# The last down projection of each MLP in seven products instead of eight, with six more adding transfers a layer and the two gate products behind it computed side by side

## The chip, the cores and the metric

One core of a Trainium2 chip runs the whole program. The metric is the device time of one execution, in microseconds (us). The kernel before was executed three times for its time: 1659.44, 1661.74 and 1659.78 us, a median of 1659.78 us. One further execution was recorded by the hardware profiler: all rows shown here come from it.

Five engines work beside each other: TensorE (PE) does matrix products and loads their weights (PEld), VectorE (DVE), ScalarE (ACT) and GpSimd (POOL) work on elements, and SyncE (SP) starts the transfers from memory. POOL's queue starts transfers too, here those that add to what lies at their destination. Each engine runs its own list of instructions in order, and waits where an instruction needs something that another engine has not finished.

## The reference

Two requests of 512 and 256 tokens go through two encoder layers with the same weights. Layer 0 mixes tokens by windowed attention, layer 1 by a gated short convolution. Behind either mixer stand an MLP with squared ReLU and a gated input embedding:

```python
for i in range(DEPTH):                       # DEPTH = 2, D_MODEL = 1024, D_FF = 4096
    ...                                      # x = x + attention or short convolution
    h = rms_norm(x, norm_mlp[i])
    x = x + jnp.square(jax.nn.relu(h @ mlp_w_up[i])) @ mlp_w_down[i]
    gate = jax.nn.sigmoid(rms_norm(x, norm_ple[i]) @ ple_w_gate[i])
    x = x + (p[i] @ ple_w_proj[i]) * gate    # p[i]: 256 features per token
return rms_norm(x, final_norm)
```

Everything is float32. The change lies in the end of the MLP, `... @ mlp_w_down[i]`, and in the beginning of `gate`, in both layers.

## The kernel before

**Layout.** The activations lie transposed: `x(m)`, m = 0..7, is a tile of 128 features by 768 tokens (both requests side by side). `H` = 384 is half the tokens, and a matmul of the MLP has 128 x 128 weights and 384 columns. A product in float32 is made from high and low parts: the high part is a copy in the shorter type fp32r (written by ACT), the low part is the difference to the original (usually a subtraction by DVE). Three matmuls stand for one: high x high, high x low of the activations, low of the weights x high.

**MLP.** The 4096 hidden rows are cut into 8 groups of 512. A group has two *up chunks* (`up`, u = 0..15), and two halves of a *down* projection (`down(g, h)`), h naming the half of the output rows. The jobs run up 0, up 1, then for each group up, down half 0, down half 1, up, so that the down projection of a group stands two chunks behind its up projection. The last job is `last_down`, group 7.

**Seven products.** Up chunks and the down projections of groups 0 to 6 cut a product of 2 x 2 blocks into seven block products instead of eight. Their keys are `w11, s3, s2, w12, s1, w22, s4`: `w` keys are blocks of the weights, `s` keys are sums of blocks (`sums32`, `sums14`, on DVE). `QS7` gives the activations that each meets (blocks or sums as well, made by `Acts`: `highx`, `lowx`, `t13`, `t42`, `high`, `low`). `product7` issues one product into one PSUM bank: in a down half a key takes 12 matmuls, six for each of its two banks. Results of one key are used twice: into another bank by a copy on ACT (`copies`: banks `A` into `C` behind w11, `A` into `B` behind s2), where the next key then accumulates. `added` in `down` adds the finished banks to `x` on DVE.

**Weights.** `Weights7` fetches two chunks of the weights (`wraw`, 512 KB each, by SP) for one half, makes high parts on ACT (`high`) and low parts on DVE (`low`; `split` does both). For the key w22 alone the low part is made without DVE (`added` of `Weights7`, line 446): ACT copies the high part negated, and a transfer on POOL's queue adds the original from memory to it. Tiles named `whi`, `wlo` have two buffers, `vhi`, `vlo` (w22) and `zhi`, `zlo` (s3 and s2) one, as have the two sums.

**The last group.** `last_down` does the whole of group 7 without the scheme: the activations of the two last up chunks are kept as they are (`whole`), four chunks of weights are fetched and split one after the other (`weight`), and each gives two output blocks of 24 matmuls: 192 matmuls of 384 columns a layer, all at line 131. Each finished block is added to `x(m)`, and `nxt.block` begins the next norm with it: ACT makes the scaled high part `xs_ple`, DVE the low part, ACT the square, DVE its running sum.

**The gates.** In layer 0 `ple` goes through eight gate products `gate` over all 768 tokens, each with its own 512 KB of weights. Behind the first stands the sum of squares over the 128 rows (a matmul), from which `rstd_ple` comes, and then for each gate a chain of DVE and ACT steps adds its part to `x`. In layer 1 `last_ple` does the same for 512 tokens first and 256 behind them, with the weights kept, and ends with the final norm. The first two gates stand ahead of the sum of squares there.

**What sets the order.** Inside the MLP the lists of ACT, PE and DVE are written by hand (`manual_schedule`): an instruction runs in the order in which the code names it. `late()` takes the next deferred step from a list (`pend`), which spreads the work on the activations of a chunk over the next chunk. Transfers on SP and POOL start in the order of the code as soon as their buffers are free.

Of the kernel before, what the change touches and what calls it, by code (L numbers as in the profile page):

```python
# [18 lines left out]
P = 128  # L19
D = 1024  # L20
KB = D // P
# [26 lines left out]
def trunk_kernel(ctx: ExitStack, tc: tile.TileContext, a: dict, out: bass.AP):  # L48
# [124 lines left out]
    class Norm:  # L173
# [4 lines left out]
        def __init__(self, i, name, places, acc, rstd=None):  # L178
            self.i, self.name, self.places, self.rplace = i, name, places, rstd
            self.xs = [], []  # L180
            self.acc = slot(acc, f"acc_{name}", F32)[:, : self.n]

        def block(self, m, xb):
            g = gain(self.i, m)
            hi, lo = (slot(self.places[8 * p + m], f"xs_{self.name}") for p in range(2))
            self.xs[0].append(hi[:])
            self.xs[1].append(lo[:])
            act.activation(hi[:], xb, AF.Copy, scale=g)
            dve.scalar_tensor_tensor(lo[:], xb, g, hi[:].bitcast(F32), ALU.mult, ALU.subtract)
            self.square(m, xb)  # L190
# [214 lines left out]
    class Weights7:  # L405
# [44 lines left out]
        def added(self, group):  # L450
# [6 lines left out]
            nc.gpsimd.dma_start(lo[:], src[:, src.shape[1] - lo.shape[1] :], accum_op=ALU.add)  # L457

# [586 lines left out]
    def mlp(l, norm, nxt, w, places, early, product=None, begun=None):  # L1045
# [14 lines left out]
        def acts_of(u, y1, y2, rest):  # L1060

            own = places[7 * (u % 2) : 7 * (u % 2) + 7]
            e = Acts(y1, y2, own, groups[u // 2], u % 2)
            if u < 2 * NG - 2:
                return [
                    lambda: squared(rest),
                    lambda: e.highx(0),
                    lambda: (e.highx(1), e.lowx(0), e.lowx(1), e.t13()),
                    e.t42,
                    lambda: e.high(0),  # L1070
                    lambda: e.high(1),
                    lambda: e.low(0),
                    lambda: e.low(1),
                ]

            def whole(i, q):
                hi, lo = slot(own[2 * i], "act"), slot(own[2 * i + 1], "act")
                split(hi[:], lo[:], q[:])
                groups[u // 2].setdefault("whole", {})[u % 2, i] = hi[:], lo[:]

            return [lambda: squared(rest), lambda: whole(1, y2), lambda: whole(0, y1)]
# [22 lines left out]
        def up_begun(u, w, make, then):  # L1104
# [71 lines left out]
        def up_plain(u, w, make, then):  # L1176
# [91 lines left out]
        def up(u, w, make, then):  # L1268


            first = u == PLAIN[l]
# [25 lines left out]
            if seven:  # L1297
                v.sums14()
                v.high("s32")
# [7 lines left out]
            rectified(y1, c, 0, H, ALU.max)  # L1307
            late()
            if seven:
                v.low("direct")  # L1310
            else:
                v = [then(0)]
# [8 lines left out]
            pend.extend(acts_of(u, y1, y2, y1))  # L1321
            return v

        def down(g, h, w, make, then):

            xg = groups[g]
            top, low = ([x(4 * h + 2 * i + s) for s in range(2)] for i in range(2))

            def products(ts, key, start):
                for s, t in enumerate(ts):  # L1330
                    product7(t, w, key, xg, start, 2 * P, s * P)
# [10 lines left out]

            w.low("s32")
# [9 lines left out]
            b = [bank("B", "b")[:, :H] for _ in range(2)]  # L1353
            products(b, "s3", True)
            p = big("p")
            for i in range(2):
                act.activation(p[:, i * H : i * H + H], b[i], AF.Copy)
            products(a, "s2", False)
            d = copies("B", a)
            for i in range(2):  # L1360
                t = low[i].rearrange("p (a n) -> p a n", a=2)
                q = p[:, None, i * H : i * H + H].broadcast_to([P, 2, H])
                dve.tensor_tensor(t, t, q, ALU.subtract)
# [621 lines left out]
```

## Time and profile before

| What | Value |
|---|---|
| median of three executions | 1659.78 us (1659.44 to 1661.74) |
| profiled execution | 1661.51 us |
| its span, first to last instruction | 1659.5 us |
| mean granted TensorE clock | 0.996 |
| matmuls on PE | 9414 |
| last down of layer 0 | about 749.9 to 783.3 us |
| its gates (`ple`) | from 783.3 us |
| last down of layer 1 | about 1543.2 to 1576.8 us |
| its gates (`last_ple`) and the end | from 1576.8 to 1659.5 us |

In rows of the profile the engine's name is followed by the line of the code, the operation and `out<-in` with the shape of each; `x12` is a count. A bracket `[1.07 <-ACT xs L312]` says that the engine had waited 1.07 us ahead of the instruction, and for which instruction of which engine. In a table of stretches each row gives the start and end, the length, and then the busy time of PE, PEld, DVE, ACT and POOL with the number of instructions, the granted clock in parts of full speed, the mean busy share of the transfer engines and GB/s. Groups of instructions show busy time, mean ns of one, and the idle time ahead of them. A row of transfers gives the queue, the count, the size and the us from issue to landing.

### The profile page before, as it was taken

The page shows a single profiled execution, that of the slowest core. Times are in us where ns is not written, and L with a number is a line of the kernel's source. Part 1 is how long each engine was busy: PE and PEld are TensorE (multiplying, and loading weights), DVE is VectorE, ACT ScalarE, POOL GpSimd, SP SyncE. Part 2 cuts the span into 40 slices and gives each one's busy share as a digit, 9 for nine tenths or more (in the row PEclk, how much of TensorE's full clock was granted, in tenths as well). Part 3 has the DMA queues.
Part 4 walks back from the last instruction along what each step waited for, and adds up shares of the span by engine and source line. Part 5 has one row for each costly group of instructions (what it writes and reads, how often), then busy time and mean ns, then how long its engine had stood idle before and what let it go on. Part 6 is the DMA issues. An engine that isn't in the chain of part 4 may idle for free.

```text
span 1659.5 us, 24297 instructions
## 1 busy us (share of the span) xinstructions
PE 1637.6 (99%) x9414; PEld 1587.3 (96%) x9414; DVE 1380.8 (83%) x2242; ACT 948.5 (57%) x1508; POOL 71.7 (4%) x104
## 2 busy tenths in 40 slices
PE   8999999999999999999999999999999999999997
PEld 7988789999999999999999999999999999999986
DVE  7598888898889889877888777778889888988776
ACT  7377766865556556545654434555555655655554
POOL 0211000000000000000000000000000000000000
PEclk9999999999999999999999999999999999999998
DMA  8755322443233333242312222112333323333222
GB/s 267 199 154 149 87 64 83 121 109 87 83 86 96 96 96 91 71 122 69 98 62 77 76 77 76 64 64 73 87 96 96 95 87 79 90 96 108 69 87 99
DMA packets 55476, 161.11 MB, mean 97 GB/s; under 512 B 7056, under 2 KB 10128, under 8 KB 55360
## 3 DMA queue, kind: packets, MB, share of 16 engines
q1 hardware_dynamic: 45184, 139.89, 26.4%
q0 software_dynamic: 10176, 19.67, 6.7%
q8 instruction: 74, 1.21, 0.3%
q14 instruction: 42, 0.34, 0.1%
HBM read 138.82 MB, written 10.48 MB: 90 GB/s over the span
## 4 chain that ended last, share of the span: by engine, by line
PE 88%; DVE 7%; ACT 4%; issue 1%; DMA 0%; DVEq 0%; SPq 0%; ACTq 0%
PE a L486 33%; PE mm L131 10%; PE mm L140 8%; PE b L486 8%; PE d L486 5%; PE c L486 5%; PE B L486 4%; PE C L486 4%; PE gate L140 3%; PE pt L760 1%; PE p L1096 1%; PE p L1199 1%; PE gate L131 1%; PE O L770 1%; PE O L771 1%
## 5 line engine op out<-in xcount | busy, mean ns | idle before, releaser
L486 PE MATMUL a<-xs,whi 128*128 128x384 f32 x624 | 121.8, 337 | 0.0
L444 ACT ACTIVATE vhi<-wraw 128x512 fp32r<-128x512 f32 x67 | 42.2, 631 | 132.3 <-PE B L486 87.9
L486 PEld LDWEIGHTS a<-xs,whi 128*128 128x128 f32 x624 | 110.0, 188 | 0.2 <-DVE y L1306 0.2
L486 PE MATMUL a<-t,zhi 128*128 128x384 f32 x536 | 109.1, 337 | 0.0
L486 PE MATMUL a<-t,whi 128*128 128x384 f32 x536 | 108.8, 336 | 0.0
L486 PE MATMUL b<-t,zhi 128*128 128x384 f32 x536 | 108.7, 336 | 0.0
L1341 DVE TENSOR_TENSOR x<-x,a 128x384 f32<-128x384 f32 x112 | 62.1, 554 | 55.3 <-PE a L486 55.3
L486 PE MATMUL a<-act,whi 128*128 128x384 f32 x448 | 96.5, 337 | 0.0
L486 PEld LDWEIGHTS a<-t,whi 128*128 128x128 f32 x536 | 94.9, 188 | 0.0
L486 PEld LDWEIGHTS b<-t,zhi 128*128 128x128 f32 x536 | 94.9, 188 | 0.0
L486 PEld LDWEIGHTS a<-t,zhi 128*128 128x128 f32 x536 | 94.8, 188 | 0.0
L464 DVE TENSOR_TENSOR wlo<-wraw,whi 128x1024 fp32r<-128x1024 f32 x70 | 85.2, 1218 | 7.9 <-ACT whi L444 7.9
L444 ACT ACTIVATE whi<-sum 128x1024 fp32r<-128x1024 f32 x67 | 70.6, 1054 | 27.0 <-PE a L486 22.7
L464 DVE TENSOR_TENSOR wlo<-sum,whi 128x1024 fp32r<-128x1024 f32 x67 | 81.8, 1220 | 5.1 <-ACT whi L444 5.1
L1058 ACT ACTIVATE y<-y 128x768 f32<-128x768 f32 x64 | 53.7, 839 | 54.4 <-DVE y L1055 54.3
L464 DVE TENSOR_TENSOR zlo<-sum,zhi 128x1024 fp32r<-128x1024 f32 x67 | 81.5, 1217 | 0.0
L140 PE MATMUL mm<-xs_mix,whi 128*128 128x512 f32 (+1 forms) x320 | 81.0, 341 | 0.0
L486 PEld LDWEIGHTS a<-act,whi 128*128 128x128 f32 x448 | 79.8, 188 | 0.0
L444 ACT ACTIVATE whi<-wraw 128x1024 fp32r<-128x1024 f32 x72 | 75.7, 1051 | 7.0 <-PE C L486 7.0
L444 ACT ACTIVATE zhi<-sum 128x1024 fp32r<-128x1024 f32 x67 | 70.9, 1058 | 11.9 <-DVE sum L420 11.0
L486 PE MATMUL a<-xs,wlo 128*128 128x384 f32 x312 | 67.1, 336 | 0.0
L358 ACT ACTIVATE t<-y 128x768 fp32r<-128x768 f32 x56 | 45.7, 838 | 34.9 <-DVE y L349 34.4
(345 smaller groups left out, 4558.4 us busy)
## 6 DMA issues: line engine op xcount, KB each, us to landing
wraw<-in_up SPq DMA_DIRECT2D x64, 512.0 KB, 3.9
wraw<-in_down SPq DMA_DIRECT2D x64, 512.0 KB, 4.2
wraw<-in_w_in SPq DMA_DIRECT2D x24, 512.0 KB, 3.5
wraw<-in_gate SPq DMA_DIRECT2D x16, 512.0 KB, 3.4
vlo<-in_up POOLq DMA_DIRECT2D x28, 256.0 KB, 5.6
vlo<-in_down POOLq DMA_DIRECT2D x28, 256.0 KB, 6.0
pj<-pjs SPq DMA_DIRECT2D x16, 384.0 KB, 2.8
wraw<-in_w_q SPq DMA_DIRECT2D x8, 512.0 KB, 4.6
```

The lines of the kernel that those rows point to most:

```text
L131: pe.matmul(t, lhsT=w, rhs=x[:, o:e], start=first and i == 0 and j == 0, stop=last and i == n - 1 and j == 2)
L140: pe.matmul(ps[:, o:e], lhsT=w, rhs=x[:, o:e], start=i == 0 and j == 0, stop=i == n - 1 and j == 2,)
L358: act.activation(t[0][:], (self.q1, self.q2)[i][:], AF.Copy)
L444: act.activation(hi[:], src, AF.Copy)
L464: dve.tensor_tensor(lo[:], src, hi[:].bitcast(F32), ALU.subtract)
L486: pe.matmul(ps, lhsT=a, rhs=b, start=start and i == 0, stop=i == len(terms) - 1, skip_group_check=True)
L760: pe.transpose(pt[:, h * P : (h + 1) * P], lg[h // 2][:, h % 2, b * P : (b + 1) * P], ident[:],)
L770: pe.matmul(O[:], lhsT=v, rhs=ph[:], start=b == 0, stop=False)
L771: pe.matmul(O[:], lhsT=v, rhs=pl[:], start=False, stop=b == nk - 1)
L1058: act.activation(t[:], t[:], AF.Square)
L1096: pe.matmul(ps[o], lhsT=wt[:, c], rhs=xs[f"x{h + 1}{1 + o}"][m][part], start=k == 0 and j == 0, stop=k == KB - 1 and j == 2,)
L1341: dve.tensor_tensor(t[:, o : o + H], t[:, o : o + H], f, op)
```

## The change

`last_down` is gone. Group 7 becomes two more halves of the seven products, written out in two new functions, `down_first` (half 0) and `down_last` (half 1), with an order of their own. The activations of the last two chunks are made by `Acts` as elsewhere, those of chunk 15 inside the last `up` and the first half. A layer does 2 x 7 x 12 = 168 matmuls there.

- The order of the keys in both halves is w11, w12, s3, s2, s1, w22, s4 (an ordinary half has w11, s3, s2, w12, s1, w22, s4).
- Inside a key the matmuls go chunk by chunk of the activations, over both banks in turn: four with the first chunk's high and low part, two with the low part of the weights, then the second chunk, which has the weights' low part first and the activations' low part last. Before, one bank was finished and then the other.
- `down_first` has the weights for its half prepared by the last `up`; the low part for w11 and w12 is subtracted by DVE late in that `up`.
- Low parts by adding transfers, in both layers: the sum for s3 and s2 of half 0 (`sum_added`, from the sum itself), w11 and w12 of half 1 (`v.added("direct")`), w22 of both halves, and the whole weights of the first two gates (`weight_added`). Those of w22 are 256 KB, the four others 512 KB.
- Each block's `xs_ple` high and low part is made as its `x(m)` becomes final: blocks 0 to 3 while half 1 runs, 6 behind its key w22, then 7, 4 and 5. `nxt.block` is cut into `high`, `low` and `square` for that.
- `first_gates` computes the two first gates side by side: blocks 0 to 3 of the first gate, then of the second, then blocks 6 and 7 of both, then 4 and 5. The sum of squares stands ahead of the second gate's last part in layer 0, and behind the third gate in layer 1. `ple` and `last_ple` take over from there.
- `last_ple` has its kept weights and outputs in other slots, and begins with gate 2.

The core of the diff:

```diff
+        def down_first(w, make, top, low, products, copies, added, third, less):
+            e = aside.pop()
+            a = [bank("A", "a")[:, :H] for _ in range(2)]
+            products(a, "w11", True)
+            e.lowx(1)
+            c = copies("C", a)
+            act.activation(e.q1[:, H:], e.q1[:, H:], AF.Square)
+            e.t13()
+            e.high(0)
+            e.t42()
+            products(c, "w12", False)
+            e.low(0)
+            e.high(1)
+            e.low(1)
+            w.split("s14")
+            v = make()
+            p = third()
+            v.added("direct")
+            added(top, 0, c, ALU.add)
+            products(a, "s2", False)
+            d = copies("B", a)
+            v.sums32()
+            v.sums14()
+            v.high("s32")
+            products(a, "s1", False)
+            added(low, H, a, ALU.subtract)
+            products(d, "w22", False)
+            v.added("w22")
+            added(low, 0, d, ALU.subtract)
+            v.low("s32")
+            products(a, "s4", False)
+            def rest():
+                added(top, H, a, ALU.add)
+                v.split("s14")
+                less(p)
+            return v, rest
+
+        def down_last(w, before, top, low, products, copies, added, third, less):
+            def part(m):
+                nxt.high(m, x(m))
+                nxt.low(m, x(m))
+            src = [a["gate"][l, PAIRED[m] if l == 0 else m] for m in range(2)]
+            t = [bank("A", "a")[:, :H] for _ in range(2)]
+            products(t, "w11", True)
+            before()
+            c = copies("C", t)
+            part(0)
+            products(c, "w12", False)
+            part(1)
+            ws = [weight_added(src[0])]
+            part(2)
+            p = third()
+            part(3)
+            added(top, 0, c, ALU.add)
+            products(t, "s2", False)
+            d = copies("B", t)
+            ws.append(weight_added(src[1], "z"))
+            less(p)
+            products(t, "s1", False)
+            added(low, H, t, ALU.subtract)
+            ...
+            products(d, "w22", False)
+            added(low, 0, d, ALU.subtract)
+            products(t, "s4", False)
+            nxt.high(6, x(6))
+            added(top, H, t, ALU.add)
+            nxt.low(6, x(6))
+            for m in (7, 4, 5):
+                part(m)
+            for m in (2, 3, 6, 7, 4, 5):
+                nxt.square(m, x(m))
+            return ws
+
+    def weight_added(src, tag="w"):
+        raw = fetch(src)
+        pool, bufs = (wp, 2) if tag == "w" else (more, 1)
+        ...
+        act.activation(hi[:], raw[:], AF.Copy)
+        act.activation(lo[:], hi[:].bitcast(F32), AF.Copy, scale=-1.0)
+        nc.gpsimd.dma_start(lo[:], src, accum_op=ALU.add)
```

and in the last `up`, with `final` for chunk 15:

```diff
-                v.high("s32")
+                (v.sum_added if final else lambda: v.high("s32"))()
...
+            if final:
+                e = chunk_acts(u, y1, y2)
+                act.activation(y1[:, :H], y1[:, :H], AF.Square)
+                e.highx(0)
             late()
-            if seven:
+            if final:
+                e.lowx(0)
+            elif seven:
                 v.low("direct")
...
             squared(y2)
+            if final:
+                e.highx(1)
+                v.low("direct")
             product7(a, w, "s4", xs, False)
```

`third` is the key s3 with the copies `p` of its two banks, `less` subtracts them from `x`.

PE in layer 0, from the end of the last up chunk (`xs` are the norm's activations of the up projection) into the down projection, before:

```order
L486 MATMUL a<-xs_3503,wlo 128x384
L486 MATMUL a<-xs_3651,wlo 128x384
L131 MATMUL mm<-act,whi 128x384 x4
L131 MATMUL mm<-act,wlo 128x384 x2
```

and now, with the end of w11 (banks `a`), the whole of w12 (banks `C`) and the first matmuls of s3 (banks `b`, weights `zhi`):

```order
L1363 MATMUL a<-act,whi 128x384
L1363 MATMUL a<-act,wlo 128x384
L1363 MATMUL a<-act,whi 128x384 x2
L1363 MATMUL C<-act,whi 128x384 x4
L1363 MATMUL C<-act,wlo 128x384 x2
L1363 MATMUL C<-act,whi 128x384
L1363 MATMUL C<-act,wlo 128x384
L1363 MATMUL C<-act,whi 128x384
L1363 MATMUL C<-act,wlo 128x384
L1363 MATMUL b<-t_7906,zhi 128x384
```

The product into `C` now stands directly behind the one into `a` of which ACT has to copy `C` first; in an ordinary half two products lie between.

ACT in an ordinary half (group 6 of layer 0), from the copies of w11's banks to those of s2's:

```order
L1336 ACTIVATE C_7759<-a_7745 128x384
L1357 ACTIVATE p_7778<-b_7764 128x384
L1357 ACTIVATE p_7778<-b_7765 128x384
L1336 ACTIVATE B_7793<-a_7744 128x384
L1336 ACTIVATE B_7794<-a_7745 128x384
```

and in the first half of group 7 of layer 0 now, between the same copies `p` and `B`:

```order
L1387 ACTIVATE p_8092<-b_8078 128x384
L1387 ACTIVATE p_8092<-b_8079 128x384
L449 ACTIVATE whi_8095<-wraw_8072 128x1024
L460 ACTIVATE wlo_8096<-whi_8095 128x1024
L1375 ACTIVATE B_8114<-a_8024 128x384
L1375 ACTIVATE B_8115<-a_8025 128x384
```

The high part of the other half's w11 and w12 and its negation have come between the copies `p` and the copies into `B`, which PE needs for s1 and w22.

ACT in the second half in layer 1, around the copies of w11's banks (`gw`, `gwr` are parts of the kept gate weights, `xs_ple1` blocks of the next norm):

```order
L449 ACTIVATE whi_15663<-sum_15553 128x1024
L84 ACTIVATE gw_15893<-wraw_15891 128x768
L1375 ACTIVATE C_15669<-a_15647 128x384
L1375 ACTIVATE C_15670<-a_15648 128x384
L186 ACTIVATE xs_ple1_15673<-x_3327,vec_76 128x768
L186 ACTIVATE xs_ple1_15689<-x_3327,vec_76 128x768
```

A copy of a gate's weights has moved ahead of the copies into `C`; it needs a chunk that SP fetches when a buffer of `wraw` is free.

More of the change, by code (lines that the diff above doesn't have):

```diff
@@ L1475, in ple @@
         for i in range(5):
[L1476 to L1477 removed]
+            gp = gps[i] if i < 2 else product(PAIRED[i], weights(i))
+            r = norm.rstd(psum, ss) if r is None else r
             for step in steps(i, gp):
@@ L1569, in last_ple @@
         y = {m: ys[m // 3][:, m % 3, :] for m in range(KB)}
-        outs = [more.tile([P, CH], F32, tag=tag, name="o", bufs=1) for tag in ("sum0", "sum1", "zhi", "zlo")]
+        outs = []
         left = list(range(KB))
```

230 lines of the change are left out of this document (139 added, 91 removed).

## The prediction

> **What bounds the kernel now.** I read the head of the page first, for what is busy and what ended last.
>
> ```profile
> span 1659.5 us, 24297 instructions
> PE 1637.6 (99%) x9414; PEld 1587.3 (96%) x9414; DVE 1380.8 (83%) x2242; ACT 948.5 (57%) x1508; POOL 71.7 (4%) x104
> PE 88%; DVE 7%; ACT 4%; issue 1%; DMA 0%; DVEq 0%; SPq 0%; ACTq 0%
> ```
>
> TensorE (PE) works 99% of the span and carries 88% of the chain that ended last. A busy share is an average, so the next view is the table of stretches around the place of the change: the last down projection of each layer, and one gate product behind the first of them.
>
> ```profile
> 750.00:783.10 33.10, 33.10 (x192) 33.10 (x191) 24.50 (x33) 18.13 (x23) 0.00 (x0) 1.00 0.21 73
> 800.60:817.40 16.80, 16.80 (x98) 16.80 (x98) 15.76 (x23) 11.78 (x16) 0.00 (x0) 1.00 0.36 103
> 1543.20:1576.80 33.60, 33.60 (x194) 33.58 (x193) 25.92 (x35) 19.78 (x25) 0.00 (x0) 1.00 0.25 82
> ```
>
> The columns after the length are PE, weight loads, DVE, ACT and POOL; then the granted clock. In both down projections PE is busy in every microsecond at full clock, with DVE and ACT at 55 to 77%. So here every matmul left out is time won, and every wait put in is time lost, one for one. The chain in order of time gives the unit prices.
>
> ```profile
> 730.98 2.11 PE B L486 x12
> 749.93 33.38 PE mm L131 x192
> 1543.23 33.53 PE mm L131 x192
> ```
>
> **What is removed.** The old stage is 192 matmuls of 384 columns in each layer, 33.38 and 33.53 us. The new one is two halves of seven products of 12 matmuls, 168 in all. A product of 12 takes 2.11 us in the seven-product stages, so a layer is 14 x 2.11 = 29.5 us without waits. Removed: 33.38 + 33.53 - 2 x 29.5 = **7.9 us**. The gate products only change places: 96 matmuls of 384 columns in layer 0, 48 of 512 in layer 1, before and after.
>
> **What is added: turns.** In an ordinary half, ACT copies the product w11 into the C banks while PE runs s3 and s2, so C is ready long before w12 needs it:
>
> ```profile
> 722.43 0.86 PE L486 MATMUL b<-t,zhi 128*128 128x384 f32 x4
> 722.63 0.47 ACT L1336 ACTIVATE C<-a 128x384 f32<-128x384 f32 x1 [0.57 <-PE a L486]
> 726.62 0.86 PE L486 MATMUL C<-act,whi 128*128 128x384 f32 x4
> ```
>
> The copy begins 0.20 us after PE has turned to the next product, takes 0.47, and PE comes back to C only at 726.62. The changed order runs w12 straight behind w11, and s1 straight behind s2 (whose banks `a` the copies into B must have read first). So PE waits out the copy. The restart is priced by a wait that the trace does have:
>
> ```profile
> 858.10 0.51 PE L1771 MATMUL c<-xs,zhi 128*128 128x384 f32 x2
> 857.81 1.02 DVE L313 SCALAR_TENSOR_TENSOR xs<-x,vec,xs 128x768 fp32r<-128x768 f32 x1 [1.07 <-ACT xs L312]
> 858.88 0.62 PE L1771 MATMUL c<-xs,zhi 128*128 128x384 f32 x2 [0.27 <-DVE xs L313]
> ```
>
> DVE ended at 858.83, PE began 0.05 later, and its first pair took 0.62 instead of 0.51: 0.11 for getting going. A bare turn is thus 0.20 + 0.47 + 0.05 + 0.11 = 0.83; the two column blocks are now interleaved, so the first bank is complete one matmul (0.17) earlier: **0.66 us**. The second bank's copy ends 0.4 later, while PE does two matmuls of the first: nothing more. Behind a waiting PE stand only its own products, and DVE's adds to x, which have slack.
>
> Turns behind a loaded ACT cost more. ACT's prices:
>
> ```profile
> L444 ACT ACTIVATE whi<-wraw 128x1024 fp32r<-128x1024 f32 x72 | 75.7, 1051 | 7.0 <-PE C L486 7.0
> L455 ACT ACTIVATE wlo<-whi 128x1024 fp32r<-128x1024 f32 x2 | 2.1, 1060 | 0.1
> L188 ACT ACTIVATE xs_ple<-x,vec 128x768 fp32r<-128x768 f32 x16 | 15.0, 938 | 29.0 <-DVE x L869 28.9
> L1357 ACT ACTIVATE p<-b 128x384 f32<-128x384 f32 x56 | 27.2, 489 | 18.1 <-PE b L486 18.1
> L390 ACT ACTIVATE act<-y 128x384 fp32r<-128x384 f32 x28 | 14.5, 516 | 0.4
> ```
>
> First half, s2 to s1: `v.added("direct")` puts a copy of 1024 columns and its negation, one needing the other, between the copies p and the copies into B. From the end of s3: 0.20 + 0.2 (the s14 high part is still running) + 0.38 + 0.38 (two p, 0.1 apart from their length since ACT overlaps) + 1.05 + 0.03 + 0.96 until B can begin, 0.47 + 0.05 until PE restarts: 3.7 us, against 2.1 that s2 fills. With 0.11: **1.7 us**. Second half: ACT must wait for w12's end to overwrite the weights (buffers `whi`), then does 1.05 + 1.06, two `xs_ple` at 0.84 apart and two p at 0.38 until B begins: 0.20 + 4.5 + 0.47 + 0.05 = 5.2 us, against 4.2 of s3 and s2. **1.1 us** with the restart. In layer 1 an extra copy `gw` stands ahead of the C copies and needs a gate chunk that is fetched only when the vhi copy has freed its buffer. That is about 3.4 us before the turn, and such fetches land after
>
> ```profile
> DMA to landing us min/median/max: 3.4/3.5/5.9
> ```
>
> so the copy starts as the turn is due and adds about 0.8 (from 0.7 at 3.4 us to 3.2 at 5.9). I take the median.
>
> **What is added: the low half of w11.** Its DVE subtraction now stands behind a longer run: y2 from s1, y1, then ACT's square and copy, the low part of x11, y2's other half, the rectification, and only then the 1024-column subtraction.
>
> ```profile
> 745.80 0.56 DVE L1306 TENSOR_TENSOR y<-a,p 128x384 f32<-128x384 f32 x1 [5.98 <-PE a L486]
> 748.45 0.96 DVE L1055 SCALAR_TENSOR_TENSOR y<-y,rstd_mlp 128x768 f32<-128x768 f32 x1
> L464 DVE TENSOR_TENSOR wlo<-wraw,whi 128x1024 fp32r<-128x1024 f32 x70 | 85.2, 1218 | 7.9 <-ACT whi L444 7.9
> ```
>
> From 745.80: 0.47 + 0.55 + 0.52 + 0.52 + 0.55 + 0.5 + 0.96 + 1.22 = 751.1. PE enters w11 at 749.77, does four high matmuls (0.70) and needs it at 750.5: **0.7 us** with the restart.
>
> **The added transfers.** Per layer six low parts (four of 512 KB, two of 256 KB) are now made by a negated copy and an adding transfer on POOL's queue. Their nearest rows:
>
> ```profile
> wlo<-in_up POOLq DMA_DIRECT2D x2, 512.0 KB, 6.1
> t<-q POOLq DMA_DIRECT2D x2, 384.0 KB, 3.9
> DMA to landing us min/median/max: 4.1/5.7/7.8
> ```
>
> The last row is that of the 256 KB ones. Laid against the new order, the zlo made from the sum has 10 us until s3 needs it, both vlo over 9, the second half's wlo 7.4, the gates' 9.9 and 8.9; in layer 1, where a gate's first four blocks take 2.8 us instead of 4.2, the second gate's zlo has 6.5. At 6.1 all land in time: nothing. At 7.8 two are late by 0.4 and one by 1.3: 2.1 us.
>
> **The gates.** Two side by side leave the blocks that come last to the end: their high and low parts are ready 3 us before PE asks. But the sum of squares goes from behind the first gate to the end of the second, so rstd comes some 6.5 us later than now:
>
> ```profile
> 796.20 0.96 DVE L270 SCALAR_TENSOR_TENSOR rstd_ple<-v,y 128x768 f32<-128x768 f32 x1
> ```
>
> PE's cover is the third gate and the free bank pairs. DVE then starts its gate work late at 94% load (15.76 of 16.80 above). Laying its rows out, the weights' low part for the fifth gate is ready 4.9 us before use and that for the sixth 1.4: nothing. A lag longer by 3 us would cost some 1.6. The second sequence's end of layer 1 keeps its order; its chain moves with PE.
>
> **The sum.** Layer 0: 0.7 + 0.66 + 1.7 + 0.66 + 1.1 = 4.8; layer 1: 5.6. Together 10.4, a further 0.3 for waits of 0.05 at the low parts of s3: **10.7 added, 7.9 removed, +2.8 us**. The profiled execution took 1661.51 (span 1659.5 and 2.0 around it), so it would take 1664.3. It stood 1.7 above the median 1659.78; a median comes to **1662.6**.
>
> **The rivals.** *Only bare turns count.* If ACT and DVE hide more than I see (a shorter queue ahead of B, w11's low half in time), four bare turns per layer stay: 8 x 0.66 = 5.3 against 7.9, so -2.6: 1657.2. For it: both have slack on average. Against: the orders are fixed by hand, and the prices are measured. *Full gain.* The seven products bring what they say, -7.9: 1651.9. It needs copies that take no time; no row shows that.
>
> *The clock falls, slower.* One stretch of the trace shows the price:
>
> ```profile
> 202.48 0.79 PE L140 MATMUL mm<-aos,whi 128*128 128x512 f32 x1 [1.56 <-DVE aos L85]
> 198.40:202.00 3.60, 2.37 (x10) 1.38 (x9) 3.48 (x13) 2.42 (x5) 0.00 (x0) 1.00 0.65 170
> 202.00:205.60 3.60, 3.12 (x8) 2.58 (x9) 3.60 (x12) 2.21 (x10) 0.00 (x0) 0.53 0.44 172
> ```
>
> PE was 66% busy over 3.6 us, with one wait of 1.56, and the next 3.6 us ran at a clock of 0.53: about 1.7 us lost. The new wait of 1.6 before s1 is as long, once in each layer; if it decides, +2.8 + 3.4 = +6.2: 1666.0. Against: the matmuls around it are dense, where those of 198 to 202 were thin. The Trainium skill (TensorE: Matmul & The Clock Gate, What's actually happening) has the clock halved after an idle window of about 3.4 us. By that no wait of this change is long enough and the sum stays; the row above, with 1.56 us, speaks for less being enough, so the rival keeps its chance. *Late low parts, slower.* Transfers at 7.8 us: +2.8 + 2.1 = +4.9: 1664.7. For it: POOL's transfers now run beside gate fetches. It decides from 7.4 us (6.5 in layer 1).
>
> **How the numbers follow.** A measurement of this kernel can tell about 0.2% (3.3 us) from no change: faster is below 1656.5, slower above 1663.1. My forecast, 1662.6 give or take 2, has 0.48 (0.36 within, 0.12 above); only bare turns 0.17 (0.14 within, 0.03 faster); full gain 0.05; the clock 0.15; late parts 0.15 (0.04 within). So faster 0.08, same 0.54, slower 0.38. The range leaves out the full gain and the outer tails: 1657.0 to 1666.5.
>
> **What would show it.** PE's waits, none of which stands there now: ACT into C four times at about 0.5, ACT into B four times at 1.0 to 1.6, DVE into w11's low half twice at 0.6; PE's matmul count down by 48. Wrong, if C waits are absent (turns hidden), if POOL transfers appear as what PE waits for, if the granted clock dips behind a B turn, or if PE waits for DVE in the third to sixth gate.

## The result, and the profile after

The changed kernel is slower: a median of 1669.91 us (1668.11 to 1671.8, five runs) against 1659.85 (1659.44 to 1662.25, five runs), a ratio of 1.0058 with a 95% interval of 1.0048 to 1.0069. The forecast was 1662.6 with a range up to 1666.5: slower was forecast, but by 2.8 and not by 10.1. The profiled execution took 1668.11 (span 1666.3). First the head of its page and its chain by engine:

```profile
span 1666.3 us, 24336 instructions
PE 1631.0 (98%) x9366; PEld 1576.3 (95%) x9366; DVE 1406.9 (84%) x2286; ACT 979.6 (59%) x1562; POOL 82.5 (5%) x116
PE 84%; DVE 8%; ACT 5%; issue 1%; DMA 1%; DVEq 0%; SPq 0%; ACTq 0%; POOLq 0%
```

PE has 48 matmuls less and 6.6 us less work, and the span is 6.8 us longer: the time went into waits. The two down projections, in the stretches that the prediction showed of before:

```profile
750.00:783.10 33.10, 30.05 (x166) 28.23 (x165) 26.44 (x38) 23.43 (x35) 4.47 (x5) 1.00 0.64 156
1543.20:1576.80 33.60, 27.62 (x150) 25.49 (x150) 26.19 (x37) 23.56 (x36) 3.57 (x4) 1.00 0.56 138
```

In both down projections PE was busy in every microsecond; now it stands still for 3 and for 6 us, while DVE and ACT have more to do. The granted clock is still 1.00 there, in this execution. Who is waited for is told by the waits of PE over the whole trace (engine, line, who waited for what; sum, times, longest):

```profile
PE a L1363 <- ACT B L1375: 4.5, 4, 1.4
PE C L1363 <- ACT C L1375: 3.9, 4, 2.7
PE gate L1558 <- DMA zlo<-in_gate: 1.7, 1, 1.7
...
PE gate L131 <- ACT whi L84: 1.4, 1, 1.4
PE a L1363 <- DVE wlo L477: 1.2, 2, 0.6
...
PE gate L131 <- DVE wlo L85: 0.4, 1, 0.4
```

None of these six stood in the kernel before. The first and the fifth were forecast, and of the second all but more than half of its longest wait, the 2.7; the 1.7 and the 1.4 with its 0.4 were not. Of the signs of being wrong that the prediction names, one came: a transfer on POOL's queue appears as what PE waits for.

To put a length to each stage, here is the distance from the first matmul of a stage to the first of the next, read from PE's rows in order of time (us). "Gates 1" are the gates of the first 512 tokens of layer 1, and the figures are good to 0.05. The other kernels are told below, under the names of the rows.

| | until down 0 | down 0 | gates 0 | rest of layer 1 | down 1 | gates 1 | end |
|---|---|---|---|---|---|---|---|
| before | 749.77 | 33.38 | 67.66 | 692.26 | 33.52 | 45.35 | 37.56 |
| after | 748.01 | 34.68 | 69.96 | 692.45 | 36.97 | 47.30 | 36.93 |
| after_again | 750.23 | 34.63 | 69.96 | 692.46 | 39.66 | 47.33 | 36.93 |
| e1 | 750.12 | 37.06 | 70.24 | 692.44 | 39.47 | 45.35 | 36.98 |
| e2 | 747.31 | 33.80 | 69.97 | 692.47 | 39.72 | 48.95 | 36.98 |
| e4 | 748.42 | 34.64 | 69.95 | 692.45 | 34.66 | 45.30 | 37.48 |
| f1 | 750.45 | 32.89 | 70.23 | 692.47 | 32.81 | 45.27 | 36.98 |
| f2 | 748.50 | 33.67 | 69.97 | 692.51 | 33.72 | 45.30 | 36.93 |
| f3 | 750.49 | 31.05 | 70.23 | 692.47 | 30.92 | 45.27 | 37.47 |
| g1 | 750.82 | 31.05 | 70.23 | 692.46 | 30.95 | 45.59 | 36.96 |
| g2 | 750.12 | 31.10 | 67.65 | 694.47 | 30.95 | 45.27 | 37.44 |
| g12 | 750.43 | 31.04 | 67.65 | 694.84 | 30.92 | 45.45 | 36.97 |
| g3 | 750.54 | 31.09 | 71.46 | 690.88 | 30.95 | 45.27 | 36.99 |

The stage until down 0 is not touched. Two things vary there from execution to execution: its first 20 us, by up to 3, and the stretch near 203 us, which runs at half clock in some traces, 1.7 us longer, as in that of before. The end varies by 0.5 with the place at which the last stretch at half clock begins: some 10 to 10.7 us ahead of the end of the span in the traces with 37.4 or more, 7 to 8 in those with 36.9 or 37.0. Without that stage the changed kernel loses 8.6 us in its first trace and 11.2 in its second: 1.3 and 1.3 in down 0, 2.3 and 2.3 in gates 0, 3.4 and 6.1 in down 1, 2.0 and 2.0 in gates 1, 0.2 in the rest of layer 1, less 0.6 at the end. The medians say 10.1.

### The profile page after: what moved, and what is told of

The parts are those of the page before. It is cut to its first block, busy times and chain, and to the rows that moved or that the text cites. A ratio compares the mean times of both kernels' runs of the same rounds, so it can differ in the third digit from the quotient of the medians.

```text
span 1666.3 us, 24336 instructions
## 1 busy us (share of the span) xinstructions
PE 1631.0 (98%) x9366; PEld 1576.3 (95%) x9366; DVE 1406.9 (84%) x2286; ACT 979.6 (59%) x1562; POOL 82.5 (5%) x116
## 4 chain that ended last, share of the span: by engine, by line
PE 84%; DVE 8%; ACT 5%; issue 1%; DMA 1%; DVEq 0%; SPq 0%; ACTq 0%; POOLq 0%
PE a L499 32%; PE mm L140 8%; PE b L499 8%; PE mm L131 6%; PE d L499 5%; PE c L499 5%; PE B L499 4%; PE C L499 4%; PE gate L140 2%; PE gate L1558 1%; PE pt L773 1%; PE a L1363 1%; PE p L1103 1%; PE p L1206 1%; PE O L783 1%
## 5 line engine op out<-in xcount | busy, mean ns | idle before, releaser
L1380 DVE TENSOR_TENSOR x<-x,a 128x384 f32<-128x384 f32 x128 | 70.2, 554 | 57.2 <-PE a L499 55.2
L449 ACT ACTIVATE whi<-sum 128x1024 fp32r<-128x1024 f32 x71 | 74.8, 1054 | 28.7 <-PE a L499 22.7
L477 DVE TENSOR_TENSOR wlo<-sum,whi 128x1024 fp32r<-128x1024 f32 x71 | 86.7, 1221 | 5.5 <-ACT whi L449 5.5
L449 ACT ACTIVATE whi<-wraw 128x1024 fp32r<-128x1024 f32 x76 | 79.8, 1051 | 7.1 <-PE C L499 7.1
L449 ACT ACTIVATE zhi<-sum 128x1024 fp32r<-128x1024 f32 x71 | 75.1, 1058 | 12.1 <-DVE sum L425 10.8
L363 ACT ACTIVATE t<-y 128x768 fp32r<-128x768 f32 x64 | 52.5, 839 | 43.4 <-DVE y L354 42.2
```

The lines of the kernel that those rows point to most:

```text
L363: act.activation(t[0][:], (self.q1, self.q2)[i][:], AF.Copy)
L449: act.activation(hi[:], src, AF.Copy)
L477: dve.tensor_tensor(lo[:], src, hi[:].bitcast(F32), ALU.subtract)
L1380: dve.tensor_tensor(t[:, o : o + H], t[:, o : o + H], f, op)
```

## The experiments

**The changed kernel again.**

> The changed kernel once more, for a second trace of it. Theory W (the loss is PE's new waits, each paid once): the same waits at the same places as in the first trace, within 0.3 us each: ACT into C 0.4, 0.4, 0.4 and 2.7, ACT into B 1.4 and 0.9 in each layer, DVE low part of w11 0.6 twice, the transfer of the second gate's low part 1.7 in layer 1, and 1.4 + 0.4 at the last gate of layer 0; span 1666 to 1668 us and a granted clock of 1.00 behind the waits. Theory C (the waits also cost clock): stretches of 3 to 4 us at about half clock right behind the waits of 1.4 to 2.7 us, 1.7 us lost each, which would fill the distance from the 1668.1 of the first trace to the median of 1669.9.

Measured: 1669.96 (ratio 1.0054, 1.0042 to 1.0067). All waits stand at the same places; the one before w12 in the second half of layer 1 is 3.9 instead of 2.7. And there is a stretch at half clock right behind it. A table of stretches of 3.41 us, of this trace:

```profile
1564.74:1568.15 3.41, 3.00 (x18) 2.68 (x16) 3.16 (x5) 1.21 (x2) 0.90 (x1) 1.00 0.74 196
1568.15:1571.56 3.41, 0.00 (x0) 0.00 (x0) 1.90 (x3) 1.19 (x3) 0.00 (x0) 1.00 0.41 77
1571.56:1574.97 3.41, 3.33 (x10) 3.33 (x11) 2.77 (x4) 2.39 (x5) 0.00 (x0) 0.50 0.00 0
```

The column before the last two is the granted clock. In the middle stretch PE does nothing, in the next it runs at 0.50, ten matmuls instead of about twenty: 1.7 us lost. So both theories are right in part: the waits stand where they stood, each paid once, and the longest also costs clock, in this trace and not in the first. The 3.9 is outside the 0.3 that theory W allowed.

**The second half in an ordinary order.** The edit, in the second half's function:

```diff
             c = copies("C", t)
             part(0)
-            products(c, "w12", False)
-            part(1)
-            ws = [weight_added(src[0])]
-            part(2)
             p = third()
-            part(3)
-            added(top, 0, c, ALU.add)
+            part(1)
             products(t, "s2", False)
             d = copies("B", t)
-            ws.append(weight_added(src[1], "z"))
+            ws = [weight(src[0], KB, tag="z")]
+            part(2)
+            products(c, "w12", False)
+            added(top, 0, c, ALU.add)
+            ws.append(weight_added(src[1]))
+            part(3)
             less(p)
```

> Second half of the last group in the order of an ordinary half (w11, s3, s2, w12, s1, w22, s4); the first gate's weights then go to the buffers zhi and zlo with a subtraction on DVE, the second gate's to whi and wlo with the adding transfer. Theory W: the two turns of that half vanish from PE's waits in both layers, C 0.4 and B 0.9 in layer 0 (1.9 us with getting going), C 2.7 and B 0.9 in layer 1 (4.2 us), of which up to 1.2 comes back because the copies into C still stand behind the gate weight's copy gw, and the wait of 1.7 for the second gate's transfer: about 6.5 us less than the changed kernel, 1663 to 1664. Rival L (in layer 0 DVE's chain behind the last product, not PE, sets when the next layer can begin): the 1.9 of layer 0 comes back as a longer wait at the last gate or the first products of layer 1; about 4.7 us less.

Measured: 1672.93 (1.0062, 1.0049 to 1.0074), no gain where 6.5 was expected. The two turns are gone, and in layer 1 1.5 of the wait behind `gw` comes back ahead of s2, near the 1.2 that was expected. But PE now waits for DVE ahead of s4, 2.4 us in layer 0 and 3.1 in layer 1. First the PE row of layer 0, then DVE's rows ahead of it:

```profile
783.51 1.65 PE L1363 MATMUL a<-act,whi 128*128 128x384 f32 x4 [2.40 <-DVE x L1380]
780.24 1.02 DVE L190 SCALAR_TENSOR_TENSOR xs_ple<-x,vec,xs_ple 128x768 fp32r<-128x768 f32 x1 [0.61 <-ACT xs_ple L186]
781.18 1.82 DVE L1394 TENSOR_TENSOR x<-x,p 128x768 f32<-128x768 f32 x2
782.91 1.01 DVE L1380 TENSOR_TENSOR x<-x,a 128x384 f32<-128x384 f32 x2
```

DVE must read s1's banks `a` (the last row) before s4 may go on in them, and stands first behind the low part of block 3, for which ACT was late, and behind the subtraction of `p`. The order that I wrote for DVE was the fault, not the order of the products. A stretch at 0.50 follows here as well, in both layers; that of layer 0:

```profile
779.93:783.34 3.41, 1.19 (x7) 0.86 (x5) 3.10 (x4) 1.74 (x3) 0.75 (x1) 1.00 1.03 290
783.34:786.75 3.41, 3.24 (x10) 3.24 (x11) 2.38 (x5) 1.46 (x2) 0.00 (x0) 0.50 0.34 66
```

**The low part of w11 earlier.** In the last `up`:

```diff
                 e.highx(0)
+                v.low("direct")
             late()
...
                 e.highx(1)
-                v.low("direct")
```

> The subtraction that makes the low part of w11 and w12 stands on DVE ahead of the low part of x11 instead of behind the rectification of y2; DVE has a gap of 1.15 us there. Theory W: both waits of 0.6 for that low part vanish, with getting going 0.87 us each: 1.7 us less than the changed kernel. Rival L: in layer 0 nothing is won, 0.9 us less in all, since the time returns at the last gate.

Measured: 1669.18 (1.0047, 1.0033 to 1.0061), 0.8 less than the changed kernel beside it, with five runs of each that overlap. Both waits of 0.6 are gone. In layer 0 the down projection is 0.85 shorter and the gates behind it are unchanged, so that rival L falls for this edit; that its 0.9 in all is near the measured 0.8 is chance. In layer 1 this trace shows no gain (down 1 at 39.72 against 39.66), because the wait before w12 in the second half is 4.5 here: the chunk for `gw` was fetched as much earlier as PE came, but took 6.7 us to land instead of 4.9 and 6.1 in the two traces of the changed kernel. Two stretches run at half clock, 6.8 us from 1565.59, around that wait, and 3.4 from 1589.48, behind the wait of 1.8 for the second gate's transfer, which makes the gates 1.65 longer.

**The gate weights' copy behind the copies into C.**

```diff
-        full=xs1[17:] + act1[:1],
-        rest=[act1[4], act1[1], act1[11], act1[2]],
-        prs=[act1[3], act1[5], act1[6]],
+        full=act1[3:4] + xs1[17:],
+        rest=[act1[0], act1[1], act1[11], act1[2]],
+        prs=[act1[4], act1[5], act1[6]],
```

> Only the places of four buffers of the end of layer 1 are exchanged, so that the first kept gate weights' copies gw and gwr stand behind the copies into C on ACT. Theory W: the wait of 2.70 us ahead of w12 in the second half of layer 1 falls to the bare turn of 0.39: 2.3 us less than the changed kernel. Rival: the wait was for ACT's copies and not for the fetch; then it stays above 1.2. If the kept weights come late by this, waits of PE for gw in the gates of layer 1.

The edit exchanges the places of four buffers; ACT's first copy `gw` then stands at 1577.8, behind the copies into C and into B. Measured: 1664.83 (1.0025, 1.0017 to 1.0034), about 5 less, where 2.3 was expected. ACT's rows of the changed kernel show why. ACT ended at 1564.50, waited for the gate chunk, and only then copied `a` into C:

```profile
1563.44 1.06 ACT L449 ACTIVATE whi<-sum 128x1024 fp32r<-128x1024 f32 x1 [0.79 <-PE a L1363]
1566.93 0.84 ACT L84 ACTIVATE gw<-wraw 128x768 fp32r<-128x768 f32 x1 [2.42 <-DMA wraw<-in_gate]
1567.68 0.85 ACT L1375 ACTIVATE C<-a 128x384 f32<-128x384 f32 x2
```

Without `gw` in that place, the waits of PE from 1500 us to 1640 in e4 are:

```profile
PE a L1363 <- ACT B L1375: 2.2, 2, 1.4
PE C L1363 <- ACT C L1375: 0.8, 2, 0.4
PE a L1363 <- DVE wlo L477: 0.6, 1, 0.6
```

The 2.7 fell to the bare turn, the 1.7 for the second gate's transfer is gone too, which no theory had said, and no stretch runs at half clock behind them. The chunk for `gw` took 5.4 us to land here, longer than in the first trace: the gain is from the place of the copy, not from a faster fetch. Of the distance to the second trace of the changed kernel, 5.0 lies in down 1 (3.5 of it the shorter wait, the rest the clock) and 2.0 in the gates.

**The second half again, with another order for DVE.** e4 and, in place of e1's order:

```diff
             d = copies("B", t)
+            less(p)
+            ws = [weight(src[0], KB, tag="z")]
+            nxt.high(2, x(2))
             products(c, "w12", False)
             added(top, 0, c, ALU.add)
+            ws.append(weight_added(src[1]))
+            nxt.high(3, x(3))
             products(t, "s1", False)
             added(low, H, t, ALU.subtract)
+            nxt.low(2, x(2))
+            nxt.low(3, x(3))
```

> The four buffers of e4 exchanged, and the second half in the ordinary order again (w11, s3, s2, w12, s1, w22, s4), now with DVE's steps in an order in which none stands behind an ACT step that comes later: the copies p are subtracted right behind s2, the low parts of blocks 2 and 3 stand behind the addition of s1's banks. Theory W+C (PE's new waits are paid once each, and a wait of more than about 2 us is followed by 3.4 us at half clock): without the DVE waits of 2.4 and 3.1 of the first attempt no wait of that half is left; both last down projections come to 34.65 - 1.9 = 32.8 us, no stretch at half clock behind them; 3.7 less than e4, about 1661. Rival S (the order of the second half is bound to ACT or DVE whatever the order): some wait of 1 us or more ahead of s1, w22 or s4 stays, and the down projections stay at 34 or more.

Measured: 1663.07 (1660.27 to 1663.4; ratio 1.0010, 1.0001 to 1.0019). Both down projections stand at 32.9 and 32.8, as theory W+C said, with no wait left in the second half. The median is 2 above the expectation; its trace has the half clock near 203 us, over 500 us ahead of the edit, as the trace of the kernel before has, whose runs beside this one had a median of 1661.81.

**The direct low part by DVE.** e4 and, in the first half:

```diff
             p = third()
-            v.added("direct")
             added(top, 0, c, ALU.add)
             products(a, "s2", False)
             d = copies("B", a)
+            v.high("direct")
...
             added(low, H, a, ALU.subtract)
+            v.low("direct")
             products(d, "w22", False)
```

> The four buffers of e4 exchanged, and in the first half the low part of the next w11 and w12 made by DVE's subtraction instead of the negated copy and the adding transfer; ACT then has the copies into B ahead of that high part. Theory W: the wait ahead of s1 in the first half falls from 1.43 to a bare turn of 0.4 in both layers, 1.05 less each: down projections of 33.6, 2.1 less than e4, about 1662.7. Rival: ACT's copies were late for another reason, or DVE's extra 1.2 us makes a later step late; then no less than e4.

Measured: 1662.43 (1.0008, 0.9999 to 1.0017); down projections of 33.67 and 33.72, so 0.97 and 0.94 less than e4. Theory W holds to a tenth.

**All of it together.** e2, e4, f1 and f2 in one kernel.

> All of it: the low part of w11 first (e2), the direct low part by DVE (f2), the second half in the ordinary order (f1), the four buffers (e4). Theory W: of PE's waits in the last down projection only the bare turns of the first half are left (C 0.4 and B 0.4 a layer); each down projection takes 29.5 + 1.4 = 30.9 us against 33.4 and 33.5 before; the gates of layer 0 still 2.3 above before. Span without stretches at half clock 1659.5 - 1.7 - 2.5 - 2.6 + 2.3 = 1655.0, 1657 with the 2 us around it: faster than the kernel before by some 0.15%. Rival L: DVE's chain through the gates of layer 0 takes back what the down projection of that layer gains; then the gates of layer 0 take 72 us or more and the median is 1659 or more.

> f3_all once more beside it, on the same chip: down projections of 31.0 and 30.9 us, gates of layer 0 of 70.2, and a ratio to the kernel before of 0.997 to 0.999, as before.

Measured: 1657.62 (1656.24 to 1659.7; ratio 0.9982, 0.9973 to 0.9990), and again 1658.65 (0.9984, 0.9975 to 0.9993): faster than both kernels. Down projections of 31.05 and 30.92. PE's waits from 740 to 870 us:

```profile
PE gate L131 <- ACT whi L84: 1.6, 1, 1.6
PE a L1363 <- ACT B L1375: 0.5, 1, 0.5
PE c L1926 <- DVE xs L318: 0.4, 1, 0.4
PE gate L131 <- DVE wlo L85: 0.4, 1, 0.4
PE C L1363 <- ACT C L1375: 0.4, 1, 0.4
```

The two bare turns of the first half are left, and the waits at the last gate, which are no smaller. So rival L falls: the gates of layer 0 keep what they lost (70.2 against 67.7 before), but of the 3.6 that the down projection gains on the changed kernel they take back 0.3.

**What makes the last gate wait.** Two edits of f3, and both together.

> f3_all with the sum of squares behind the last down projection freed of two pieces of DVE's work: the squares of blocks 2 and 3 are added while the second half still runs, and the third gate's low part in layer 0 is made by the adding transfer. Theory R (rstd comes too late after the change, DVE works without a gap from there on, and PE pays at the last gate of layer 0): rstd_ple of layer 0 comes about 1.8 us earlier against the start of the gates, the waits at the last gate (1.6 and 0.4, 2.3 with getting going) fall below 0.5, the gates of layer 0 take 68.2 instead of 70.2, and the median is about 2 below f3_all, 1655.6. Rival: the last gate waits for ACT's order of steps, not for the lag; then its wait stays within 0.3.

> f3_all with the weights of the last gate of layer 0 prepared before the sixth gate's sigmoid instead of behind its block, so that PE finds them in time. Theory R (the lag is in the DVE chain): the wait at the last gate goes, and up to all of it returns at the first products of layer 1, whose wait for DVE's xs grows from 0.4 to about 2; less than 0.7 us less than f3_all. Rival (ACT's order of steps alone made that wait): the 2.3 us are won, gates of layer 0 at 68.0 and layer 1 still at 692.5; about 1655.4.

> Both edits. By theory R: as g1_rstd_earlier or a little less, 1655.5, with no wait at the last gate and 0.4 to 0.8 at the first products of layer 1. By the rival: as g2_last_gate_weights, 1655.4.

g1 adds the squares of blocks 2 and 3 earlier and makes the third gate's low part by an adding transfer; g2 moves one line:

```diff
-            for step in steps(5, gp):
-                step()
-            w7 = weights(7)
+            times, sigmoid, added, block = steps(5, gp)
+            times()
+            w7 = weights(7)
+            sigmoid()
+            added()
+            block()
```

Measured: g1 1659.3 (0.9988, 0.9979 to 0.9997), a miss: rstd began 20.2 us behind the start of the gates, as in f3, because the sum of squares has its fixed place on PE, and the wait stayed at 1.6. g2 1659.09 (0.9986, 0.9978 to 0.9995): the gates take 67.65, and layer 1 takes 2.0 more, 694.47, since the wait moved to its first products:

```profile
PE c L1929 <- ACT xs L317: 1.8, 1, 1.8
```

So it is no matter of one step's place: ACT and DVE, taken together, are late there. Both edits together gave 1658.26 (0.9983, 0.9974 to 0.9992), like f3, where 1655.5 was expected.

> As g1_rstd_earlier (squares early in layer 0 alone), and the sum of squares of layer 0 also stands earlier on PE, ahead of the last block of the first gate instead of behind it; in g1 rstd_ple had stayed 20.2 us behind the start of the gates, tied to PE's place of that sum. Theory R: rstd_ple now begins about 18 us behind the start of the gates, the wait at the last gate of layer 0 falls from 1.6 by about as much as rstd gains, to 0 to 0.6, and the gates of layer 0 take 68 to 69 with the first products of layer 1 unchanged (layer 1 at 692.5): 1.5 to 2 less than f3_all. Rival (the pace of the gates, not their beginning, makes the lag): the wait at the last gate stays at 1.3 or more although rstd comes earlier.

g3 has the sum ahead of the last block of the first gate. Measured: 1659.69 (0.9985, 0.9976 to 0.9994). rstd came 2.1 us earlier (18.1 behind the start of the gates), and the wait at the last gate fell only from 1.6 to 1.3: the rival was right, theory R fell. The gates take 71.46 in this trace, since a stretch at half clock (1.7 us) begins behind that wait, and the rest of layer 1 is 1.6 shorter, since PE comes to its first products later and no longer waits there; together they take 0.4 less than in f3. Where the lag may come from is seen in DVE's work in the 58 us from the start of the gates, before, after, and in f3:

```profile
783.15:841.15 58.00, 58.00 (x334) 58.00 (x334) 48.58 (x67) 36.23 (x46) 0.00 (x0) 1.00 0.28 89
782.69:840.69 58.00, 58.00 (x334) 58.00 (x334) 52.22 (x70) 38.11 (x49) 0.00 (x0) 1.00 0.30 95
781.54:839.54 58.00, 58.00 (x334) 58.00 (x334) 52.42 (x72) 39.16 (x49) 0.00 (x0) 1.00 0.30 94
```

DVE (the number in front of its count, 48.58 before) has 3.6 us more to do in the same stretch: four more additions of squares and two more low parts, because the last four blocks all become final at the end of the second half instead of one every 4 us. In g3 it has no gap of more than 0.3 us from 809 us to 836. That this work makes the lag is argued, not shown: in g1 DVE has 1.0 less to do there than in f3, and the wait is the same. Which of its steps would have to go elsewhere was not found.

## Why the prediction was wrong, point by point

The mechanism of the turns was right. Four steps failed: the term for `gw` was too small, the second gate's transfer and the gates of layer 0 were put at nothing, and the clock was kept out of the sum.

**Right: the removed work and the waits priced from rows.** Fourteen products at 2.11: f3 with two bare turns a layer takes 31.05, that is 29.5 and 1.5. The waits of layer 0 in the changed kernel, in order:

```profile
749.46 0.62 PE L1363 MATMUL a<-act,wlo 128*128 128x384 f32 x2 [0.59 <-DVE wlo L477]
...
751.51 1.01 PE L1363 MATMUL C<-act,whi 128*128 128x384 f32 x4 [0.39 <-ACT C L1375]
...
759.70 1.00 PE L1363 MATMUL a<-t,whi 128*128 128x384 f32 x4 [1.43 <-ACT B L1375]
...
768.84 1.00 PE L1363 MATMUL C<-act,whi 128*128 128x384 f32 x4 [0.39 <-ACT C L1375]
...
776.26 0.99 PE L1363 MATMUL a<-t,whi 128*128 128x384 f32 x4 [0.85 <-ACT B L1375]
```

A bracket gives less than the loss: matmuls overlap by 0.16 (each takes 0.34, one begins every 0.174), and the first ones after a wait take 0.1 to 0.15 longer. With both, the five cost 0.87, 0.69, 1.74, 0.69 and 1.16, forecast 0.7, 0.66, 1.7, 0.66 and 1.1. Down 0 was forecast at 4.95 - 3.9 = +1.05 and came to +1.30.

**Wrong in size: the term "adds about 0.8" for the gate weights' copy `gw`.** It was worked out at 3.5 us to landing, the median of the kernel before, with 3.2 as the other end. The chunk that `gw` waits for was indeed fetched 3.4 us ahead of the turn, but it took longer. Here it is with the adding transfer that ran beside it, in the first trace of the changed kernel and then in the second:

```profile
wraw<-in_gate SPq DMA_DIRECT2D x1, 512.0 KB, 4.9
vlo<-in_down POOLq DMA_DIRECT2D x1, 256.0 KB, 5.1
```

```profile
wraw<-in_gate SPq DMA_DIRECT2D x1, 512.0 KB, 6.1
vlo<-in_down POOLq DMA_DIRECT2D x1, 256.0 KB, 6.2
```

The term was 2.3 in the first trace (2.70 against the bare 0.39), 3.5 in the second and 4.1 in e2, where the chunk took 6.7: each time the landing less 2.6, where the prediction's working takes off 2.7. So the wait was priced rightly, and the landing was not. A median of the old kernel was the wrong value for a transfer that the change itself sets among others. That the adding transfer beside it makes the fetch slow is likely but not shown, since no run took it away. The share of the down projection of layer 1 was forecast at +1.75 and came to +3.45 in the first trace and, with the slower fetch and the clock, +6.14 in the second.

**Wrong: "at 6.1 all land in time: nothing".** The second gate's zlo cost 1.7 us in layer 1. It landed after 6.8, beyond the 6.5 that the rival of late low parts named, and it was issued late, which the prediction had not laid out. The two transfers of the gates in layer 1, then their rows on POOL's queue with the negated copy ahead of the second:

```profile
wlo<-in_gate POOLq DMA_DIRECT2D x1, 512.0 KB, 6.8
zlo<-in_gate POOLq DMA_DIRECT2D x1, 512.0 KB, 6.8
```

```profile
1573.19 0.89 POOL L1538 DMA_DIRECT2D wlo<-in_gate  x1 [9.23 <-ACT wlo L1537]
1577.54 1.06 ACT L1537 ACTIVATE zlo<-zhi 128x1024 fp32r<-128x1024 f32 x1
1580.36 0.89 POOL L1538 DMA_DIRECT2D zlo<-in_gate  x1 [6.28 <-ACT gwr L84]
```

Elsewhere in this trace POOL issues 0.41 us after the copy has ended; here that would have been 1579.0. But the first transfer landed at 1580.04, and the second goes out 0.32 behind that, 1.35 late. The named releaser `gwr` only happened to end then. In e4 the second is held back in the same way, but the two took 5.6 and 5.5, so that it landed 2.4 earlier against the start of the gates, and PE did not wait; why they were faster there is open. The trace of before had shown the holding back. Three adding transfers in a row; the group's 3.9 us to landing stands in the prediction:

```profile
329.22 0.88 POOL L370 DMA_DIRECT2D t<-q  x1 [5.90 <-DVE sum L420]
333.47 0.89 POOL L370 DMA_DIRECT2D t<-q  x1 [3.37 <-issue]
337.72 0.88 POOL L457 DMA_DIRECT2D vlo<-in_up  x1 [3.36 <-issue]
```

329.22 + 3.9 = 333.1, and the next row begins 0.3 later, released by nothing that the profile names ("issue"). The prediction had laid out the slack of each transfer by itself alone.

**Wrong: "nothing" for the gates of layer 0.** That rstd comes some 6.5 us later was right (6.2). The prediction laid out DVE's rows to the sixth gate, where the slack had shrunk from 4.9 to 1.4, and stopped. The sixth was in time; the eighth was not, and it waits for ACT's high part first, which was not laid out:

```profile
843.49 0.97 PE L131 MATMUL gate<-xs_ple,whi 128*128 128x384 f32 x4 [1.38 <-ACT whi L84]
844.87 0.62 PE L131 MATMUL gate<-xs_ple,wlo 128*128 128x384 f32 x2 [0.41 <-DVE wlo L85]
```

With the restart this is the 2.3 of the gates. A slack that falls by 3.5 in one gate had to be followed to the end of the stage. What would take the lag away stays open.

**Undervalued: the clock.** The rival had 0.15, its price per stretch (1.7) was right, and its place was not: it named the waits of 1.6 before s1, of which no trace shows one that costs clock. The longer waits in layer 1 do, in some traces. The rule that the traces bear out is below. The Trainium skill (TensorE: Matmul & The Clock Gate, What's actually happening) has the clock fall after an idle window of about 3.4 us, and the windows run freely. The length and the free running agree with these traces; that the window must be idle does not: a window with 1.63 us of work was enough.

In sum, the forecast of +2.8 lacked 2.3 in gates 0, 2.0 in gates 1, and 1.7 to 4.4 in down 1. The last two belong together: a moved copy, a slow fetch, a held-back transfer and the clock, all in the same 40 us of layer 1, which the prediction had as separate terms and rivals and never added up.

## What to carry to other kernels

Where PE is the bound, two things decide what fewer products are worth: that no product stands directly behind the one whose banks must first be copied (0.7 us each here, 1.2 and 1.7 where ACT was loaded), and that no copy on which PE waits stands behind a copy that waits for a transfer. Give DVE an order in which nothing that PE needs soon stands behind a step that waits for ACT. And price a transfer that a change brings among others by the slow end of its rows, and look for the wait that it makes long enough to cost clock as well.

## What the runs showed of the hardware

**The clock is decided in windows of 3.41 us.** Each stretch at half clock lasts 3.4 us or twice that, but for the last, which runs on to the end of the trace, and the beginnings in one trace lie on a grid: in the second trace of the changed kernel at 202.81, at 1571.55, 401 times 3.413 later, and, at its end, at 1663.71, 27 times 3.413 later still. What counts is PE's work in the window before. In all fourteen traces, from 40 us on, windows with 0.00 to 1.63 us of work (0.47, 0.90, 1.19 and 1.41 among them) were each followed by one at 0.50, and none with 2.2 or more was; from 1.69 to 2.1 both were seen (g3's window of 1.84 at the last gate was followed by one). So the same wait costs clock or not by its place on the grid, and no length of wait decides it alone, such as the 2 us that the expectation of f1 names: in e2 a wait of 1.8 cost clock, and in the first trace of the changed kernel the 2.70 did not, which fell into two windows:

```profile
1563.35:1566.76 3.41, 2.15 (x13) 1.83 (x11) 3.16 (x5) 1.06 (x1) 0.61 (x1) 1.00 0.79 196
1566.76:1570.17 3.41, 1.97 (x11) 1.89 (x12) 2.46 (x3) 3.24 (x6) 0.00 (x0) 1.00 0.17 31
```

No experiment filled a wait with other matmuls, so that the clock alone was changed; that part rests on the traces.

**POOL's queue holds back an adding transfer of 256 KB or more until the one before it, of 384 or 512 KB, has landed.** It goes out 0.3 to 0.4 us behind that landing: at the gates of both layers and behind the 512 KB from the sum in both traces of the changed kernel, and at the place of 329 us in the kernel before; in no trace kept does one go out earlier. Plain transfers of 96 KB on the same queue (`bias<-skew`) go out in groups, one every 0.6 us, while earlier ones, which take some 4 us, are still under way. Whether smaller adding transfers would overlap was not tried, and why the large ones do not is not shown.
